# One matmul of 512 columns for the high and low parts of the input tokens in the last layer's feature-major products

## The chip, the cores and the metric

One core of a Trainium2 chip. The metric is the device time of one launch in microseconds (us). TensorE does the matrix products, ACT (ScalarE) and DVE (VectorE) the work on elements, SP issues the loads.

## The reference

Two layers act on 256 input tokens (x) and 256 context tokens, with 1024 features. A layer is: a gated feed-forward (hidden width 2816), a mixer with three branches, and a second feed-forward; each ends in a layer norm whose scale and shift come from a conditioning vector. In the last layer the context goes no further than the mixer's keys, values and states, so that all later products have only the 256 input tokens.

```python
for l in range(DEPTH):
    x = ffn_step(x); ctx = ffn_step(ctx)          # silu(h@a) * (h@g) @ w2
    zx, zc = split(mod(x) @ w_in), split(mod(ctx) @ w_in)
    a = gla_out(...) @ gla_proj                   # decay attention
    b = (z6 * short_conv(z7 * z8)) @ conv_proj    # short convolution over 3 tokens
    c = latent_attention(...) @ mla_proj
    x = norm(x + (sig(zg_a)*a + sig(zg_b)*b + sig(zg_c)*c) @ w_out)
    x = ffn_step(x)
```

## The kernel before

All products are made from high and low parts: a value v is split into h, its copy in the type that TensorE multiplies, and l = v - h. A product w·v is the sum wh·vh + wh·vl + wl·vh, three matmuls into the same PSUM tile (`mm3`, L227 to L235).

Weights come in tiles of 128 x 1024 values (512 KB). SP loads them in the order of use into five buffers. ACT makes the high part wh (L187) and DVE the low part wl (L188), into three buffers. The function `w` (L156), called before a tile's products, first issues the split of the tile that comes two later (`AHEAD` is 2). Nothing is reordered: each engine takes its instructions in the order in which the program issues them. An ACT or DVE operation that the program puts ahead of such a split therefore holds it back.

The activations hT are feature-major: 128 features by 512 tokens for each of 8 blocks k; columns X (0 to 255) are the input tokens, C (256 to 511) the context. `hTh` and `hTl` are two constant tiles. In the last layer, after its first feed-forward, `parts` is [X] and the products have 256 columns. `fm` (L246) runs a list of weight tiles: a tile of 256 output features by 4 blocks k has 8 pairs of output and block, so 16 products with wh and then 8 with wl. A tile for a gate has 128 outputs by 8 blocks, and as many products.

The stages of the last layer with such products, in order of time, and what follows their products:

- Gates (`gates`, L980): 3 x 8 outputs zg; ACT's tanh reads PSUM (L989). Those of latent attention fill in between its heads, those of decay attention between its outputs (`gla`), those of conv come inside its branch. The tanh is issued when the generator is next asked for a tile.
- Branches (`branch`, L992): 8 outputs each for latent attention (operand o), decay attention (yT) and conv (cv). DVE multiplies with the gate (L1010) and adds the branch before (L1012), whose rows SP loads from DRAM; in the conv branch ACT and DVE split the result (L243, L244). Beside the latent-attention branch the decays are made (L1079 to L1091, products dz).
- Conv (`conv`, L1022): four blocks of z7, z8 and z6, two outputs each. z7 is copied by ACT (L1034); z8 is multiplied by DVE (L1041), then ACT (L1043) and DVE (L1045, L1046) make the three-token filter; z6 is multiplied (L1051) and split (L240, L241).
- Feed-forward (`ffn_in`, L713): 11 blocks of four weight tiles (two for a, two for g), two outputs of each. ACT's Silu reads a (L739), DVE multiplies by g (L740), both split (L240, L241). In the block p = 1 DVE also renews the four pieces of the layer norm's result (L596, L597), one behind each weight tile.

Quantities that stay as they are: the first feed-forward and layer 0 (512 columns, `parts` is [X, C]), the mixer's first tiles, the query products, all token-major products (`tm_mm`).

Of the kernel before, what the change touches and what calls it, by code (L numbers as in the profile page):

```python
# [10 lines left out]
F32R = mybir.dt.float32r  # L11
U32 = mybir.dt.uint32
AF = mybir.ActivationFunctionType
ALU = mybir.AluOpType
# [96 lines left out]
class Core:  # L111
# [115 lines left out]
    def mm3(self, items, late):  # L227


        mm = self.nc.tensor.matmul  # L230
        for out, lhs, rhs, start, _ in items:
            mm(out, lhs[0], rhs[0], start=start, stop=False)  # L232
            mm(out, lhs[late], rhs[1 - late], start=False, stop=False)  # L233
        for out, lhs, rhs, _, stop in items:
            mm(out, lhs[1 - late], rhs[late], start=False, stop=stop)  # L235

    def split(self, hi, lo, src, scale=None):
        nc = self.nc
# [60 lines left out]
def build(ctx, tc, aps, out, plan=None):  # L299
# [200 lines left out]
        dve.tensor_scalar(ab0[:, 0, k], modT[0][:, 8 + 4 * half:12 + 4 * half, :], scalar1=1.0, scalar2=None, op0=ALU.add)  # L500
        dve.tensor_copy(ab0[:, 1, k], modT[0][:, k, :])

    hTh, hTl = g.const([P, 8, 512], "hTh", F32R), g.const([P, 8, 512], "hTl", F32R)
    hT = [(hTh[:, k, :], hTl[:, k, :]) for k in range(8)]

    def to_psum(z):

# [58 lines left out]
    def project_ln(op, nk, wsrc, tiles, l, i, gscale, inputs, keep, ab, kept=4):  # L566
# [142 lines left out]
        norm(d_)  # L709
        return [lambda: (put(c_), put(d_), onward([c_, d_]))], late  # L710


    def ffn_in(l, j, hT, tiles, gT, pend, late, opening=None):  # L713
        parts = parts_of(tiles)
        full = slice(0, parts[-1].stop)
        w13 = R["ffn_w13"][l, j]
        tiles_of = lambda c0, ps: g.fm_tiles(w13, c0, 8, g.pair_outs(ps), parts)
        psa, psg = {}, {}
        for p in range(NFB // 2):
            if p == 0 and opening is not None:  # L720
                psa[0], psg[0], psa[1] = [[g.PS("a") for _ in range(2)] for _ in range(3)]
                opening(tiles_of(0, psa[0]), tiles_of(DFF, psg[0]), tiles_of(256, psa[1]))
            else:
                tl = []
                if p not in psa:
                    psa[p] = [g.PS("a") for _ in range(2)]
                    tl += tiles_of(p * 256, psa[p])
                psg[p] = [g.PS("g") for _ in range(2)]
                tl += tiles_of(DFF + p * 256, psg[p])
                for n, _ in enumerate(g.fm(tl, hT, parts, group=3 if p == 0 and len(parts) > 1 else 1)):  # L730
                    if pend and n >= 1:
                        pend.pop(0)()
                    if late and p >= 1:
                        late.pop(0)()
                    elif p >= 2:
                        feed_share(4 * (NFB // 2 - 1 - p) + 2 - n)
            for b in range(2):
                s = g.T(name="sil")
                act.activation(s[:, full], psa[p][b][:, full], AF.Silu)  # L739
                dve.tensor_tensor(s[:, full], s[:, full], psg[p][b][:, full], op=ALU.mult)  # L740
                h, lo = g.pairs(1, "g")[0]
                g.split(h[:, full], lo[:, full], s[:, full])
                gT.append((h, lo))
        feed(10 ** 6)
# [6 lines left out]
    def mla(l, hT, tiles, W, krT, psq, o_all, filler, late):  # L751
# [202 lines left out]
        for i in range(nu + 2):  # L954
            if 1 <= i <= nu:
                live[i - 1][1]()
            if i < nu:
                hp, j, part = units[i]
                if i % (2 * np_) == 0:
                    if nxt is not None:  # L960
                        run_all(nxt)
                    nxt = heads(hp + 1, ds[hp + 1]) if hp + 1 < HM // 2 else None
                live[i] = [*score(ds[hp], j, part)]
            for _ in range((1, 2, 1, 0)[i % 4] if np_ == 2 else (3, 1)[i % 2]):
                if nxt is not None:
                    next(nxt, None)
                else:
                    next(filler, None)
            if i % (2 * np_) == 2 * np_ - 1 or i >= nu:
                next(filler, None)  # L970
            if i >= 2:
                hp, j, part = units[i - 2]
                if part is parts[0]:
                    o_all.append(g.pairs(1, "o")[0])
                values(ds[hp], j, part, live.pop(i - 2)[0], o_all[2 * hp + j])
            if 1 <= i <= nu:
                live[i - 1] = [prob_t(live[i - 1][0], units[i - 1][2])]
            renew(i % 2 == 1)

    def gates(l, bi, hT, tiles, W, zg):  # L980

        parts = parts_of(tiles)
        full = slice(0, parts[-1].stop)
        for b in range(8):
            ps = g.PS("zg")
            yield from g.fm(g.fm_tiles(W, C_ZG + bi * D + b * P, 8, [(0, P, ps)], parts, 128), hT, parts)
            th = g.U(name="th")
            f = 24 * l + 8 * bi + b
            act.activation(th[:, full], ps[:, full], AF.Tanh, scale=0.5, bias=hbg[:, f:f + 1])  # L989
            zg.append(th)  # L990

    def branch(l, op, proj, tiles, prev, outp, gts, zg, under=None, side=None):  # L992

        parts = parts_of(tiles)
        full = slice(0, parts[-1].stop)
        dst = None if outp is not None else tc.dram_tile([8, P, 512], F32, name=g.nm("mrg"))
        for p in range(4):
            while len(zg) < 2 * p + 2 and next(gts, gts) is None:
                pass
            if prev is not None:  # L1000
                pv = []
                for b in range(2):
                    u = g.U(name="prev")
                    sp.dma_start(u[:, full], prev[2 * p + b, :, full])
                    pv.append(u)
            psp = [g.PS("pj") for _ in range(2)]
            run_all(g.fm(g.fm_tiles(proj, p * 256, 8, g.pair_outs(psp), parts), op, parts), under and [under.pop(0)], 0, side)
            ms = [g.U(name="mg") for _ in range(2)]
            for b, m in enumerate(ms):
                dve.scalar_tensor_tensor(m[:, full], zg[2 * p + b][:, full], 1.0, psp[b][:, full], op0=ALU.add, op1=ALU.mult)  # L1010
                if prev is not None:
                    dve.tensor_tensor(m[:, full], m[:, full], pv[b][:, full], op=ALU.add)  # L1012
            for b, m in enumerate(ms):
                if outp is not None:
                    h, lo = g.pairs(1, "m")[0]
                    g.split(h[:, full], lo[:, full], m[:, full], 0.5)
                    outp.append((h, lo))
                else:
                    pool.dma_start(dst[2 * p + b, :, full], m[:, full])
        return dst  # L1020

    def conv(l, hT, tiles, W, side):  # L1022
# [5 lines left out]
        for p in range(4):  # L1028
            z = []
            ps = [g.PS("z7") for _ in range(2)]  # L1030
            run_all(g.fm(g.fm_tiles(W, C_Z7 + p * 256, 8, g.pair_outs(ps), parts), hT, parts), side=side)
            for b in range(2):
                t_ = g.T(name="z7")
                act.activation(t_[:, full], ps[b][:, full], AF.Copy)  # L1034
                z.append(t_)
            ps = [g.PS("z8") for _ in range(2)]
            run_all(g.fm(g.fm_tiles(W, C_Z8 + p * 256, 8, g.pair_outs(ps), parts), hT, parts), side=side)
            for b in range(2):
                y = z[b]
                u_ = g.U(name="cu")  # L1040
                dve.tensor_tensor(u_[:, full], y[:, full], ps[b][:, full], op=ALU.mult)  # L1041
                wv = lambda j: vec("conv_w", (l * 3 + j) * 8 + 2 * p + b)
                act.activation(y[:, full], u_[:, full], AF.Copy, scale=wv(1))  # L1043
                u3, y3 = r3(u_), r3(y)
                dve.scalar_tensor_tensor(y3[:, :, 1:], u3[:, :, :255], wv(0), y3[:, :, 1:], op0=ALU.mult, op1=ALU.add)  # L1045
                dve.scalar_tensor_tensor(y3[:, :, :255], u3[:, :, 1:], wv(2), y3[:, :, :255], op0=ALU.mult, op1=ALU.add)  # L1046
            ps = [g.PS("z6") for _ in range(2)]
            run_all(g.fm(g.fm_tiles(W, C_Z6 + p * 256, 8, g.pair_outs(ps), parts), hT, parts), side=side)
            for b in range(2):
                y = z[b]  # L1050
                dve.tensor_tensor(y[:, full], y[:, full], ps[b][:, full], op=ALU.mult)  # L1051
                h, lo = g.pairs(1, "cv")[0]
                g.split(h[:, full], lo[:, full], y[:, full])
                ops.append((h, lo))
        return ops

    def decay_weights(l):
# [36 lines left out]
    def gla(l, hT, tiles, W, gd, yT):  # L1094
# [128 lines left out]

        def to_yT(s):
            if not yT:
                yT.extend(g.pairs(8, "yT"))
            part = (X, C)[s]
            for k2 in range(4):
                ps = g.PS("yT")
# [249 lines left out]
```

## Time and profile before

| | us |
|---|---|
| median of 3 runs | 2694.52 (2691.72 to 2694.92) |
| profiled execution | 2696.85 |
| its span, first to last instruction | 2695.0 |
| PE busy (14243 products) | 2624.4, 97% |
| PEld busy (14243 weight loads) | 2235.4, 83% |
| DVE busy (2429 instructions) | 1601.8, 59% |
| ACT busy (1565 instructions) | 982.4, 36% |

PE is TensorE's matmuls, PEld its loads of stationary operands, which overlap with them. Matmuls are pipelined: one has a duration of 0.28 to 0.39 us, but the next starts earlier, so the rate is read from the starts. An engine's share of the span is an average over stages with different limits.

### The profile page before, as it was taken

The numbers are of one execution on the slowest core, as the hardware profiler recorded it, in microseconds if no ns is written. First come the engines' busy times: TensorE is split into PE (matmuls) and PEld (weight loads), VectorE is DVE, ScalarE is ACT, GpSimd is POOL, SyncE is SP. The second block draws the span as 40 slices with busy tenths as digits, with TensorE's granted clock in tenths as the row PEclk, the third lists the DMA queues.
The fourth block names the chain that finished last, engine by engine and source line by source line (L and its number), as shares of the span: only waits on it lengthen the run. The fifth ranks groups of instructions, "written<-read, shape, count | busy, mean of one in ns | idle before, by whom it ended". The sixth has DMA issues, their size and how long they took to land. (4 is left out here: it accounts for less than half of the span.)

```text
span 2695.0 us, 36231 instructions
## 1 busy us (share of the span) xinstructions
PE 2624.4 (97%) x14243; PEld 2235.4 (83%) x14243; DVE 1601.8 (59%) x2429; ACT 982.4 (36%) x1565; POOL 81.0 (3%) x149
## 2 busy tenths in 40 slices
PE   8999999999999999999999999998999999999998
PEld 6888789888887888878888788886789988998996
DVE  3666547765453767466666466554367745566655
ACT  2322224555332322333222142221245643454442
POOL 0000000000000000000000000000010000100000
PEclk9999999999999999999999999999999999999999
DMA  7554443223222645644454544464543343567555
GB/s 251 168 167 155 160 160 114 67 63 121 79 71 70 197 148 155 186 137 133 157 164 157 176 144 156 157 197 167 182 125 102 120 126 95 177 183 220 180 188 172
DMA packets 324609, 400.63 MB, mean 149 GB/s; under 512 B 28403, under 2 KB 241935, under 8 KB 324439
## 3 DMA queue, kind: packets, MB, share of 16 engines
q1 hardware_dynamic: 321623, 391.99, 46.3%
q0 software_dynamic: 2816, 6.34, 0.6%
q8 instruction: 111, 1.82, 0.3%
q14 instruction: 59, 0.48, 0.1%
HBM read 382.49 MB, written 15.77 MB: 148 GB/s over the span
## 5 line engine op out<-in xcount | busy, mean ns | idle before, releaser
L188 DVE TENSOR_TENSOR wl<-raw,wh 128x1024 fp32r<-128x1024 f32 (+1 forms) x529 | 638.5, 1214 | 545.6 <-ACT wh L187 348.3
L187 ACT ACTIVATE wh<-raw 128x1024 fp32r<-128x1024 f32 (+1 forms) x529 | 548.8, 1050 | 767.7 <-PE tm L233 272.9
L232 PE MATMUL a<-hTh,wh 128*128 128x512 f32 (+1 forms) x784 | 267.6, 355 | 6.9 <-DVE hTh L534 3.9
L440 DVE SCALAR_TENSOR_TENSOR acc<-raw,csil,acc 128x512 f32<-128x512 f32 x392 | 267.5, 745 | 0.0
L233 PE MATMUL a<-hTl,wh 128*128 128x512 f32 (+1 forms) x752 | 258.5, 356 | 1.5 <-DVE hTl L535 1.2
L232 PE MATMUL tm<-wh,gh 128*128 128x512 f32 x616 | 245.9, 399 | 6.6 <-ACT wh L187 6.6
L232 PE MATMUL g<-hTh,wh 128*128 128x512 f32 (+1 forms) x704 | 245.2, 359 | 0.0
L233 PE MATMUL tm<-wh,gl 128*128 128x512 f32 x616 | 243.9, 396 | 0.0
L233 PE MATMUL g<-hTl,wh 128*128 128x512 f32 (+1 forms) x688 | 240.2, 360 | 0.0
L232 PEld LDWEIGHTS a<-hTh,wh 128*128 128x128 f32 x784 | 151.8, 194 | 30.9 <-DVE hTh L534 4.8
L235 PE MATMUL tm<-wl,gh 128*128 128x512 f32 x616 | 163.4, 390 | 0.6 <-DVE wl L188 0.6
L233 PEld LDWEIGHTS a<-hTl,wh 128*128 128x128 f32 x752 | 145.6, 194 | 21.3 <-DVE hTl L535 2.8
L240 ACT ACTIVATE gh<-sil 128x512 fp32r<-128x512 f32 (+1 forms) x88 | 50.9, 578 | 302.1 <-DVE sil L740 302.1
L235 PE MATMUL a<-hTh,wl 128*128 128x512 f32 (+1 forms) x752 | 158.3, 353 | 0.8 <-DVE wl L188 0.8
L232 PEld LDWEIGHTS g<-hTh,wh 128*128 128x128 f32 x704 | 133.0, 189 | 20.7 <-issue 1.6
L235 PE MATMUL g<-hTh,wl 128*128 128x512 f32 (+1 forms) x688 | 149.5, 359 | 0.0
L232 PEld LDWEIGHTS tm<-wh,gh 128*128 128x128 f32 x616 | 118.7, 193 | 34.8 <-ACT wh L187 7.0
L233 PEld LDWEIGHTS g<-hTl,wh 128*128 128x128 f32 x688 | 130.0, 189 | 19.1
L235 PEld LDWEIGHTS a<-hTh,wl 128*128 128x128 f32 x752 | 126.6, 192 | 19.8 <-DVE wl L188 1.0
L233 PEld LDWEIGHTS tm<-wh,gl 128*128 128x128 f32 x616 | 118.5, 192 | 24.6
L235 PEld LDWEIGHTS tm<-wl,gh 128*128 128x128 f32 x616 | 115.4, 188 | 25.7 <-DVE wl L188 1.9
L235 PEld LDWEIGHTS g<-hTh,wl 128*128 128x128 f32 x688 | 117.9, 189 | 19.3
(323 smaller groups left out, 4706.3 us busy)
## 6 DMA issues: line engine op xcount, KB each, us to landing
raw<-in_ffn_w_dram SPq DMA_DIRECT2D x279, 512.0 KB
raw<-in_w_in_dram SPq DMA_DIRECT2D x156, 512.0 KB
raw<-in_ada_w_dram SPq DMA_DIRECT2D x128, 512.0 KB
raw<-in_w_out_dram SPq DMA_DIRECT2D x20, 512.0 KB
raw<-in_ada_w_dram SPq DMA_DIRECT2D x32, 256.0 KB
raw<-in_mla_proj_dram SPq DMA_DIRECT2D x16, 512.0 KB
raw<-in_gla_proj_dram SPq DMA_DIRECT2D x16, 512.0 KB
raw<-in_conv_proj_dram SPq DMA_DIRECT2D x16, 512.0 KB
```

What stands on the lines that cost most here:

```text
L187: nc.scalar.activation(hi[:, :n], raw[:, :n], AF.Copy)
L188: nc.vector.tensor_tensor(lo[:, :n], raw[:, :n], hi[:, :n].bitcast(F32), op=ALU.subtract)
L232: mm(out, lhs[0], rhs[0], start=start, stop=False)
L233: mm(out, lhs[late], rhs[1 - late], start=False, stop=False)
L235: mm(out, lhs[1 - late], rhs[late], start=False, stop=stop)
L240: nc.scalar.activation(hi, src, AF.Copy)
L440: dve.scalar_tensor_tensor(a, b, csil[:, k, s_:s_ + 1], a, op0=ALU.mult, op1=ALU.add)
```

## The change

`hTh` and `hTl` become the two halves of one tile `hT2`, so that for each block k one operand gives the 256 high and the 256 low columns of X, 512 in two runs. The operands o, yT and cv of the branches keep high and low part in one tile (`xpairs`), side by side. Where `parts` is [X], `fm_x` calls `fm_both`: wh multiplies both parts in one matmul of 512 columns, so that wh·vh is in columns 0 to 255 of the PSUM tile and wh·vl in 256 to 511; wl·vh is then added to the first half. `total` copies the second half out of PSUM with ACT and adds the first to it with DVE, and what read PSUM before reads the result from SBUF. The three products for a pair of output and block become two. The products that use `g.fm` with only X in the query path and those inside the heads stay.

```diff
+    def fm_both(self, tiles, act):
+        mm = self.nc.tensor.matmul
+        for pieces, ks, outs, nk, _ in tiles:
+            wh, wl = self.w(pieces, len(ks))
+            for c0, m, o in outs:
+                for kk, k in enumerate(ks):
+                    mm(o, wh[:, kk, c0:c0 + m], act[k][1], start=k == 0, stop=False)
+            for c0, m, o in outs:
+                for kk, k in enumerate(ks):
+                    mm(o[:, :256], wl[:, kk, c0:c0 + m], act[k][0], start=False, stop=k == nk - 1)
+            yield
+    def xpairs(self, n, name):
+        us = [self.U(F32R, name) for _ in range(n)]
+        return [(u[:, X], u[:, C], u) for u in us]
...
+    hT2 = g.const([P, 2, 8, 512], "hT2", F32R)
+    hTh, hTl = hT2[:, 0], hT2[:, 1]
+    hTx = [(hTh[:, k, X], hT2[:, :, k, X]) for k in range(8)]
...
+    def fm_x(tl, op, parts, group=1):
+        if len(parts) == 2:
+            return g.fm(tl, op, parts, group)
+        return g.fm_both(tl, hTx if op is hT else [(o[0], o[2]) for o in op])
+    def total(dst, ps, parts):
+        if len(parts) == 2:
+            return ps
+        act.activation(dst, ps[:, C], AF.Copy)
+        dve.tensor_tensor(dst, dst, ps[:, X], op=ALU.add)
+        return dst
...
-                act.activation(s[:, full], psa[p][b][:, full], AF.Silu)
-                dve.tensor_tensor(s[:, full], s[:, full], psg[p][b][:, full], op=ALU.mult)
+                a_ = total(s[:, X], psa[p][b], parts)
+                act.activation(s[:, full], a_[:, full], AF.Silu)
+                dve.tensor_tensor(s[:, full], s[:, full], total(s[:, C], psg[p][b], parts)[:, full], op=ALU.mult)
...
-            act.activation(th[:, full], ps[:, full], AF.Tanh, scale=0.5, bias=hbg[:, f:f + 1])
+            act.activation(th[:, full], total(th[:, X], ps, parts)[:, full], AF.Tanh, scale=0.5, bias=hbg[:, f:f + 1])
...
-                dve.scalar_tensor_tensor(m[:, full], zg[2 * p + b][:, full], 1.0, psp[b][:, full], op0=ALU.add, op1=ALU.mult)
+                dve.scalar_tensor_tensor(m[:, full], zg[2 * p + b][:, full], 1.0, total(m[:, X], psp[b], parts)[:, full], op0=ALU.add, op1=ALU.mult)
...
-                dve.tensor_tensor(u_[:, full], y[:, full], ps[b][:, full], op=ALU.mult)
+                dve.tensor_tensor(u_[:, full], y[:, full], total(u_[:, X], ps[b], parts)[:, full], op=ALU.mult)
...
-                dve.tensor_tensor(y[:, full], y[:, full], ps[b][:, full], op=ALU.mult)
+                dve.tensor_tensor(y[:, full], y[:, full], total(y[:, C], ps[b], parts)[:, full], op=ALU.mult)
```

## Rows read from the trace of the kernel before

**Rows 1.** Busy time by stretch: length, each engine (instructions), granted clock, DMA share, GB/s.

```profile
2135.00:2161.00 26.00, 25.43 (x203) 24.87 (x204) 20.05 (x29) 24.27 (x35) 3.34 (x6) 1.00 0.43 129
...
2416.00:2462.00 46.00, 46.00 (x386) 46.00 (x385) 29.03 (x39) 22.38 (x32) 0.00 (x0) 1.00 0.82 250
2495.00:2626.00 131.00, 130.85 (x1062) 130.34 (x1063) 76.98 (x98) 61.39 (x90) 0.00 (x0) 0.98 0.59 187
```

**Rows 2.** Timeline, feed-forward, PE: start us, duration, instruction, count [idle before <-releaser].

```profile
2566.26 1.12 PE L235 MATMUL g<-hTh,wl 128*128 128x256 f32 x8
2567.22 0.28 PE L232 MATMUL a<-hTh,wh 128*128 128x256 f32 x1
```

**Rows 3.** Timeline of PE, products of 512 columns in layer 0.

```profile
152.28 1.98 PE L235 MATMUL a<-hTh,wl 128*128 128x512 f32 x8
154.09 0.39 PE L232 MATMUL a<-hTh,wh 128*128 128x512 f32 x1
```

**Rows 4.** Timeline of PE, value products of latent attention, first and what follows.

```profile
2052.43 0.28 PE L232 MATMUL v<-wh,ckh 128*128 128x256 f32 x1
...
2055.30 0.28 PE L232 MATMUL zg<-hTh,wh 128*128 128x256 f32 x1
```

**Rows 5.** Groups by line and shape: busy us, mean ns | idle before and releaser.

```profile
L1034 ACT ACTIVATE z<-z 128x256 f32<-128x256 f32 x8 | 3.1, 384 | 6.5 <-PE z L235 6.1
...
L740 DVE TENSOR_TENSOR sil<-sil,g 128x256 f32<-128x256 f32 x20 | 8.4, 418 | 10.0 <-PE g L235 10.0
```

**Rows 6.** Timeline of DVE, ACT and PE behind a steady feed-forward block.

```profile
2567.01 0.42 DVE L740 TENSOR_TENSOR sil<-sil,g 128x256 f32<-128x256 f32 x1 [1.11 <-PE g L235]
...
2570.10 2.36 DVE L188 TENSOR_TENSOR wl<-raw,wh 128x1024 fp32r<-128x1024 f32 x2 [0.52 <-ACT wh L187]
...
2567.46 0.42 ACT L240 ACTIVATE gh<-sil 128x256 fp32r<-128x256 f32 x1 [2.55 <-DVE sil L740]
...
2568.70 0.42 ACT L240 ACTIVATE gh<-sil 128x256 fp32r<-128x256 f32 x1 [0.55 <-DVE sil L740]
2569.03 2.00 ACT L187 ACTIVATE wh<-raw 128x1024 fp32r<-128x1024 f32 x2
...
2572.98 0.28 PE L232 MATMUL g<-hTh,wh 128*128 128x256 f32 x1
```

**Rows 7.** Timeline of DVE, feed-forward block p = 1: first low part, and the multiplication.

```profile
2512.51 1.23 DVE L188 TENSOR_TENSOR wl<-raw,wh 128x1024 fp32r<-128x1024 f32 x1 [0.52 <-ACT wh L187]
...
2522.37 0.41 DVE L740 TENSOR_TENSOR sil<-sil,g 128x256 f32<-128x256 f32 x1
```

**Rows 8.** Two waits in PE's timeline, and busy time by stretch behind them.

```profile
1854.74 0.79 PE L232 MATMUL tm<-wh,gh 128*128 128x512 f32 x1 [6.60 <-ACT wh L187]
...
2312.75 0.39 PE L232 MATMUL pj<-yTh,wh 128*128 128x256 f32 x1 [1.10 <-ACT wh L187]
...
1856.00:1860.00 4.00, 4.00 (x11) 3.08 (x11) 2.60 (x4) 0.37 (x1) 0.00 (x0) 0.53 0.60 174
...
2310.00:2314.00 4.00, 2.90 (x24) 2.69 (x23) 2.63 (x5) 3.42 (x6) 0.00 (x0) 1.00 0.01 4
```

**Rows 9.** Timeline of PE, latent-attention branch, last weight tile.

```profile
2157.91 0.39 PE L232 MATMUL pj<-oh,wh 128*128 128x256 f32 x1 [0.57 <-ACT wh L187]
```

**Rows 10.** Timeline of ACT and DVE, end of decay attention.

```profile
2301.92 0.48 ACT L989 ACTIVATE th<-zg,hbg 128x256 f32<-128x256 f32 x1
...
2306.65 0.84 ACT L243 ACTIVATE yTh<-yT,hgn 128x256 fp32r<-128x256 f32 x2 [1.56 <-DVE yTl L244]
...
2311.64 2.96 ACT L187 ACTIVATE wh<-raw 128x1024 fp32r<-128x1024 f32 x3
...
2303.43 1.66 DVE L1222 SCALAR_TENSOR_TENSOR sr<-go,oss,sr 128x256 f32<-128x256 f32 x4 [5.62 <-POOL oss L749]
```

**Rows 11.** Timeline of ACT, conv branch, gate and next weight part.

```profile
2444.19 0.46 ACT L989 ACTIVATE th<-zg,hbg 128x256 f32<-128x256 f32 x1
2444.55 1.05 ACT L187 ACTIVATE wh<-raw 128x1024 fp32r<-128x1024 f32 x1
```

More of the change, by code (lines that the diff above doesn't have):

```diff
@@ L501, in mod_ab0 @@
         dve.tensor_copy(ab0[:, 1, k], modT[0][:, k, :])
-    hTh, hTl = g.const([P, 8, 512], "hTh", F32R), g.const([P, 8, 512], "hTl", F32R)
+    hT2 = g.const([P, 2, 8, 512], "hT2", F32R)
+    hTh, hTl = hT2[:, 0], hT2[:, 1]
     hT = [(hTh[:, k, :], hTl[:, k, :]) for k in range(8)]
+    hTx = [(hTh[:, k, X], hT2[:, :, k, X]) for k in range(8)]
     def to_psum(z):
@@ L710, in project_ln @@
         return [lambda: (put(c_), put(d_), onward([c_, d_]))], late
+    def fm_x(tl, op, parts, group=1):
+        if len(parts) == 2:
+            return g.fm(tl, op, parts, group)
+        return g.fm_both(tl, hTx if op is hT else [(o[0], o[2]) for o in op])
+    pairs_x = lambda n, name, parts: (g.pairs if len(parts) == 2 else g.xpairs)(n, name)
+    def total(dst, ps, parts):
[4 more added lines that the diff above has]
+        return dst
     def ffn_in(l, j, hT, tiles, gT, pend, late, opening=None):
@@ L729, in ffn_in @@
                 tl += tiles_of(DFF + p * 256, psg[p])
-                for n, _ in enumerate(g.fm(tl, hT, parts, group=3 if p == 0 and len(parts) > 1 else 1)):
+                for n, _ in enumerate(fm_x(tl, hT, parts, 3 if p == 0 else 1)):
                     if pend and n >= 1:
@@ L973, in mla @@
                 if part is parts[0]:
-                    o_all.append(g.pairs(1, "o")[0])
+                    o_all.append(pairs_x(1, "o", parts)[0])
                 values(ds[hp], j, part, live.pop(i - 2)[0], o_all[2 * hp + j])
@@ L985, in gates @@
             ps = g.PS("zg")
-            yield from g.fm(g.fm_tiles(W, C_ZG + bi * D + b * P, 8, [(0, P, ps)], parts, 128), hT, parts)
+            yield from fm_x(g.fm_tiles(W, C_ZG + bi * D + b * P, 8, [(0, P, ps)], parts, 128), hT, parts)
             th = g.U(name="th")
             f = 24 * l + 8 * bi + b
-            act.activation(th[:, full], ps[:, full], AF.Tanh, scale=0.5, bias=hbg[:, f:f + 1])
+            act.activation(th[:, full], total(th[:, X], ps, parts)[:, full], AF.Tanh, scale=0.5, bias=hbg[:, f:f + 1])
             zg.append(th)
@@ L1006, in branch @@
             psp = [g.PS("pj") for _ in range(2)]
-            run_all(g.fm(g.fm_tiles(proj, p * 256, 8, g.pair_outs(psp), parts), op, parts), under and [under.pop(0)], 0, side)
+            run_all(fm_x(g.fm_tiles(proj, p * 256, 8, g.pair_outs(psp), parts), op, parts), under and [under.pop(0)], 0, side)
             ms = [g.U(name="mg") for _ in range(2)]
             for b, m in enumerate(ms):
-                dve.scalar_tensor_tensor(m[:, full], zg[2 * p + b][:, full], 1.0, psp[b][:, full], op0=ALU.add, op1=ALU.mult)
+                dve.scalar_tensor_tensor(m[:, full], zg[2 * p + b][:, full], 1.0, total(m[:, X], psp[b], parts)[:, full], op0=ALU.add, op1=ALU.mult)
                 if prev is not None:
@@ L1030, in conv @@
             ps = [g.PS("z7") for _ in range(2)]
-            run_all(g.fm(g.fm_tiles(W, C_Z7 + p * 256, 8, g.pair_outs(ps), parts), hT, parts), side=side)
+            run_all(fm_x(g.fm_tiles(W, C_Z7 + p * 256, 8, g.pair_outs(ps), parts), hT, parts), side=side)
             for b in range(2):
                 t_ = g.T(name="z7")
-                act.activation(t_[:, full], ps[b][:, full], AF.Copy)
+                if len(parts) == 2:
+                    act.activation(t_[:, full], ps[b][:, full], AF.Copy)
+                else:
+                    total(t_[:, X], ps[b], parts)
                 z.append(t_)
             ps = [g.PS("z8") for _ in range(2)]
-            run_all(g.fm(g.fm_tiles(W, C_Z8 + p * 256, 8, g.pair_outs(ps), parts), hT, parts), side=side)
+            run_all(fm_x(g.fm_tiles(W, C_Z8 + p * 256, 8, g.pair_outs(ps), parts), hT, parts), side=side)
             for b in range(2):
@@ L1047, in conv @@
             ps = [g.PS("z6") for _ in range(2)]
-            run_all(g.fm(g.fm_tiles(W, C_Z6 + p * 256, 8, g.pair_outs(ps), parts), hT, parts), side=side)
+            run_all(fm_x(g.fm_tiles(W, C_Z6 + p * 256, 8, g.pair_outs(ps), parts), hT, parts), side=side)
             for b in range(2):
                 y = z[b]
-                dve.tensor_tensor(y[:, full], y[:, full], ps[b][:, full], op=ALU.mult)
-                h, lo = g.pairs(1, "cv")[0]
-                g.split(h[:, full], lo[:, full], y[:, full])
-                ops.append((h, lo))
+                dve.tensor_tensor(y[:, full], y[:, full], total(y[:, C], ps[b], parts)[:, full], op=ALU.mult)
+                hl = pairs_x(1, "cv", parts)[0]
+                g.split(hl[0][:, full], hl[1][:, full], y[:, full])
+                ops.append(hl)
         return ops
@@ L1225, in to_yT @@
             if not yT:
-                yT.extend(g.pairs(8, "yT"))
+                yT.extend(pairs_x(8, "yT", parts))
             part = (X, C)[s]
```

## The prediction

> **What bounds the kernel now.** I read the stages first: [rows 1] give the busy time of each engine in three stretches of the last layer. TensorE is busy for 130.85 of 131 us in the last feed-forward input and 46.00 of 46 in the conv branch, at a granted clock of 0.98 to 1.00 (the 2.4 GHz level). So the stretches that the change touches are bound by the stream of products, and a shorter stream is time won as long as the weight parts arrive in time. The latent-attention branch is different: ACT is busy 24.27 of 26 us there. Next I read the distance between products [rows 2, 3], then the waits of ACT and DVE, to see who has to finish before the weight parts of a coming tile are made, because the change lengthens just that.
>
> **The products.** Eight products of 256 columns take from 2566.26 to 2567.22, 0.120 us each [rows 2]; eight of 512 take from 152.28 to 154.09, 0.2265 us each [rows 3]. Two of 256 are 0.240, so a joined pair saves 0.0135 us, call it 0.0133: the cost that a product has beside its columns is paid once less. The new moving operand of hT is two runs of 256 lying 16 KB apart. Its nearest row is the value product, whose moving operand is two separated runs of 128: 24 of these take from 2052.43 to 2055.30, 0.120 each [rows 4], no more than one run does. I take 0.2265; the other end is 0.240, no gain at all. The pairs: 44 outputs in the feed-forward, 24 gates, 24 projections and 24 in conv, 116 outputs times 8 blocks, 928 pairs. A weight tile (8 pairs, 24 products) falls from 2.88 to 2.773 us, and 116 tiles save 12.4 us. The feed-forward's first two tiles or so run at the 1.2 GHz level (the 0.98 of [rows 1]); for these I count no saving, 0.25 us less.
>
> The Trainium skill (TensorE: Matmul & The Clock Gate, section Back-to-back issue gap) gives an isolated gap of N/2.4 + 2.5 ns, 109 and 216 ns. By it a pair saves 2.5 ns and the 928 save 2.3 us. The rows say 120 and 226.5, so I go by them.
>
> **What is added.** Each of the 116 outputs now needs an ACT copy of its low half out of PSUM and a DVE addition of the high half, before the operation that read PSUM directly; in conv 8 copies existed already. Both forms are in the trace: 0.384 and 0.418 us [rows 5]. That is about 41 us of ACT and 48 us of DVE in stretches where both have idle time. Their price lies in the order: ACT and DVE also make the weight parts, in program order, two tiles ahead.
>
> The hand-overs [rows 6]: DVE to ACT 0.45 us from start to start (multiplication 2567.01, split 2567.46), the operation and 0.03. ACT to DVE is the same (weight part of 1.06 at 2569.03, low part at 2570.10), so 0.41 behind a copy. The next independent operation on ACT comes 0.33 later (split 2568.70, weight part 2569.03), a second low part on DVE 1.13 later (two in 2.36). A dependent one on DVE I put at 0.45.
>
> *Feed-forward, steady block.* Call T the moment when the first gate output is complete: the fourth of the eight products of 2566.26 [rows 2] ends at 2566.26 + 0.36 + 0.28 = 2566.90. Now the weight part for the third tile after it starts at T + 2.13 and ends at T + 3.2; that tile starts at 2572.98, T + 6.08. After the change both outputs pass in series: copy 0.11, add 0.52, multiply 0.97, split 1.42, copy of the second a 1.75, add 2.21 (behind the low part on DVE), Silu 2.66, copy 2.95, add 3.36, multiply 3.81, split 4.26, weight part 4.59 to 5.65. The tile starts at T + 0.32 + 2 x 2.773 = 5.87. It just fits: no stall, but the slack is down from 2.9 to 0.2 us.
>
> *Feed-forward, second block.* Here DVE also does four renewals of the layer norm and is busy without a gap from 2512.51 to the multiplication at 2522.37, 9.86 us [rows 7]. In the changed kernel this run begins behind the longer chain of block one, at T + 5.67, so the first addition comes at T + 15.53, 4.4 us after that block's products are done. From there it is 0.45 to Silu, 0.29 to the copy, and 4.48 to the weight part, which ends at T + 21.8. The tile is due at T + 0.32 + 6 x 2.773 = 16.96. TensorE stands still for 4.95 us, once.
>
> *Clock.* Such a gap has a price of its own. After 6.60 us of waiting for a weight part the clock was at 1.2 GHz, still 0.53 granted in 1856 to 1860; after 1.10 us it stayed at 1.00 [rows 8]. About 5 us at half speed cost 2.5 us. Bounds: 0 and 3.4.
>
> *Latent-attention gates and branch.* The 8 gates are filler and save 0.85; I leave 0.3 of it, since each puts a DVE addition between ACT's operations. In the branch ACT is full, and a tile already waited 0.57 us for its weight part and started at 2157.91 [rows 9]. Four more copies go in front of that part, 4 times 0.33 minus some 0.43 that ACT waits there now: about 0.85 later. The tile starts that much later although it is due sooner, so the branch loses 0.7 instead of saving 0.85. The gap of some 2.3 us may lower the clock; half the cost of a short one, 0.9.
>
> *Decay-attention end and branch.* The first gate's addition is queued on DVE behind the four multiplications of 2303.43, so its tanh comes at 2305.46 instead of 2301.92 and the next weight parts 3.5 us later; the transposed outputs of 2306.65 shift by 1.9 us, and behind them the second gate passes copy and addition, so the weight part of 2311.64, for which the branch's second tile waits already (1.10 us, start 2312.75), comes 2.9 later [rows 8, 10]. Five tiles' savings are inside that wait; 11 others keep 1.2. Net +1.4, and 1.0 for the clock at a gap of 2.7 us.
>
> *Conv.* By the same hand-overs z8's two outputs, which pass ACT and DVE in series, stay in time by 0.45 with copy and addition in each. z6 comes 1.1 us late to DVE, behind two low parts, and runs eight hand-overs: the weight part ends at T + 6.1, due at 5.75, 0.45 late with TensorE's own take-up, in each of 4 blocks. Saving 2.56, loss 1.8: -0.8.
>
> *Conv branch.* Here splits, gate and weight part are one row of hand-overs (tanh 2444.19, weight part 2444.55 [rows 11]). With copies and additions a gate costs weight part 1.07, low part 1.13, addition 0.45, tanh 0.36: 3.01 against 2.773 for its products, and a block comes to about 11.8 us against 11.52 before. With the entry from conv: +1.0.
>
> **Sum.** Feed-forward -4.45 + 4.95 + 0.2 (its last block) = +0.7; latent attention -0.3 + 0.7; decay attention +1.4; conv -0.8; conv branch +1.0; clock 2.5 + 0.9 + 1.0 = 4.4. Together +7.1, of which I take 6.5, since early small slips are partly inside later ones. The profiled execution took 2696.85 (span 2695.0 and 1.85 around it), 2.33 above the median of 2694.52; so 2703.35 there and 2701.0 as a median.
>
> **Rivals.** *It cancels (2696).* The clock does not fall at any of the three gaps, and the gate rows overlap better than hop by hop: without the 4.4 and without the conv branch's 1.0 the sum is +1.7. For it: the clock stayed up after 1.10 us, and two of the three gaps lie between that and 6.60. Against it: the 4.95 us lie near the 6.60.
>
> *The stream's saving survives (2684).* If the weight parts stay ahead everywhere, only 12.2 us of saving is left, with perhaps 2 us lost: -10. One way to it: the copy need not wait for the last products, since the low half is complete 0.96 us before the high half. Against it: the high half's additions wait for the end anyway, and [rows 10] show ACT's reading of the other half of a bank ending its wait with DVE's read (2306.65), so halves are not independent. The 9.86 us run of DVE does not depend on it either.
>
> *No gain per pair (2711).* If reading two separate runs costs as much as the join saves, a pair gains nothing: 12.4 us are missing, though the weight parts then have 0.2 us more per two tiles and the losses of both conv stages (2.8) fall away: +6.5 + 12.4 - 2.8 = +16. For it: no row has runs 16 KB apart. Against it: [rows 4]. The Trainium skill's isolated gap (TensorE: Matmul & The Clock Gate, Back-to-back issue gap) would lead to the same case within some 2 us; [rows 2, 3] are against that.
>
> **Chances.** Forecast (slower, own range 2697 to 2708): 0.53, of which most lies above +5.4. Cancels: 0.26. Saving survives: 0.17. No gain per pair: 0.04. A measurement of this kernel can tell about 0.2%, 5.4 us. The range must reach into the second and third case at the bottom: 2687 to 2709. Faster 0.17; the cancelling case and the lower edge of the forecast, same 0.33; slower 0.50.
>
> **What would show it.** Right: joined products 0.2265 us apart; one gap of 4 to 6 us on TensorE in the third feed-forward block, released by an ACT weight part, with half clock behind it; ACT's weight parts in steady blocks starting 4.6 us after T; a wait above 3 us at the second tile of the decay-attention branch; conv-branch blocks of 11.8 us. Wrong: no gap above 2 us on TensorE in these stages, or additions that start before the renewals on DVE; then the time is below 2690. Distances of 0.24 us would mean the last rival.

## The result and the profile after

Before 2694.72 us (2691.72 to 2695.9, 4 runs), after 2719.44 (2718.61 to 2720.1, 4 runs): ratio 1.0093 (1.0081 to 1.0106), slower by 24.7 us where 6.5 were forecast, and outside the range. The profiled execution has a span of 2717.8 us, 22.8 more than before.

Where it went, by the start of the first product of each stage in the two timelines (a forecast for a branch includes the gates ahead of it):

| first product of | before | after | later by | lost since the row above | forecast, clock included |
|---|---|---|---|---|---|
| latent attention's gates | 2055.3 | 2053.7 | -1.6 | | |
| latent-attention branch | 2135.2 | 2140.7 | 5.5 | 7.1 | -0.3 |
| decay-attention branch | 2308.6 | 2314.7 | 6.1 | 0.6 | 1.6 |
| conv (z7) | 2347.4 | 2360.2 | 12.8 | 6.7 | 2.4 |
| conv branch | 2425.2 | 2436.5 | 11.4 | -1.4 | -0.8 |
| layer norm (zT) | 2484.4 | 2505.4 | 21.0 | 9.7 | 1.0 |
| feed-forward | 2494.8 | 2516.7 | 21.9 | 0.9 | 0 |
| end of the span | 2695.0 | 2717.8 | 22.8 | 0.9 | 3.2 |

So the loss lies in three places: latent attention's gates, the decay-attention branch and the conv branch. The stage conv itself gains. Two numbers are not the change's own: the -1.6 stands ahead of its first product, and the last 0.9 is too small by some 1.6. The low clock behind the feed-forward's first product cost 3.3 us of full-speed time in before's trace and 1.7 in after's, but also 1.7 in the trace of z3 below, which has before's products: it differs from one execution to the next.

The busy time by stretch, for the stages of [rows 1] at their new times (columns as there):

```profile
2131.00:2166.00 35.00, 30.89 (x160) 26.70 (x161) 26.50 (x43) 28.59 (x49) 3.75 (x6) 0.90 0.42 127
2438.00:2484.00 46.00, 39.70 (x205) 33.81 (x204) 27.39 (x45) 23.81 (x41) 0.00 (x0) 0.93 0.70 216
2517.00:2649.00 132.00, 127.36 (x711) 111.41 (x711) 91.07 (x137) 74.64 (x131) 0.00 (x0) 0.98 0.57 182
```

The conv branch, where TensorE was busy without a break, now has 6.3 us of 46 without a product, and a clock of 0.93. The joined products in the feed-forward, PE's timeline of after (they answer to [rows 2, 3]):

```profile
2594.50 2.00 PE L245 MATMUL a<-hT,wh 128*128 128x512 f32 x8
2596.34 1.12 PE L248 MATMUL a<-hT,wl 128*128 128x256 f32 x8
2597.30 2.00 PE L245 MATMUL g<-hT,wh 128*128 128x512 f32 x8
```

Eight joined products take 1.84 us, 0.230 each. A weight tile takes 2.79 on the mean of ten (2558.19 to 2586.12) against 2.88, so the product itself gains, a little less than forecast. The loss is in the waits of PE, here the main ones of after (in brackets the idle time and who ended it):

```profile
2114.30 2.12 PE L245 MATMUL zg<-hT,wh 128*128 128x512 f32 x8 [1.38 <-ACT wh L187]
2132.99 0.38 PE L232 MATMUL o<-pTh,vh 128*128 128x256 f32 x1 [3.11 <-ACT pTh L259]
2164.12 2.11 PE L245 MATMUL pj<-o,wh 128*128 128x512 f32 x8 [1.64 <-ACT wh L187]
2315.76 0.90 PE L245 MATMUL pj<-yT,wh 128*128 128x512 f32 x2 [0.52 <-DVE yT L263]
2317.17 1.44 PE L245 MATMUL pj<-yT,wh 128*128 128x512 f32 x5 [0.52 <-DVE yT L263]
2321.83 3.59 PE L245 MATMUL pj<-yT,wh 128*128 128x512 f32 x8 [2.27 <-ACT wh L187]
2357.11 2.11 PE L245 MATMUL pj<-yT,wh 128*128 128x512 f32 x8 [1.66 <-ACT wh L187]
2450.92 3.10 PE L245 MATMUL pj<-cv,wh 128*128 128x512 f32 x8 [2.65 <-ACT wh L187]
2479.26 3.60 PE L245 MATMUL pj<-cv,wh 128*128 128x512 f32 x8 [3.19 <-ACT wh L187]
2551.07 3.54 PE L245 MATMUL g<-hT,wh 128*128 128x512 f32 x8 [4.64 <-ACT wh L187]
```

Two smaller waits, 0.50 at 2343.72 and 0.41 at 2464.33, are left out. Three of these places were foreseen: 2321.83 (the decay-attention branch, where before waits 1.10 already), 2551.07 (the feed-forward) and 2164.12 (the latent-attention branch). Those at 2114.30, 2132.99 and 2357.11 and the two of the conv branch were not; they have two causes.

*The row of a gate.* ACT and DVE of after, two gates one behind the other in latent attention:

```profile
2126.79 0.37 ACT L746 ACTIVATE th<-zg 128x256 f32<-128x256 f32 x1
2127.65 0.51 ACT L1028 ACTIVATE th<-th,hbg 128x256 f32<-128x256 f32 x1 [0.49 <-DVE th L747]
2128.06 1.04 ACT L187 ACTIVATE wh<-raw 128x1024 fp32r<-128x1024 f32 x1
2129.01 0.36 ACT L746 ACTIVATE th<-zg 128x256 f32<-128x256 f32 x1
2130.73 0.51 ACT L1028 ACTIVATE th<-th,hbg 128x256 f32<-128x256 f32 x1 [1.36 <-DVE th L747]
2131.14 1.04 ACT L187 ACTIVATE wh<-raw 128x1024 fp32r<-128x1024 f32 x1
...
2132.35 1.07 ACT L259 ACTIVATE pTh<-pT 128x512 fp32r<-128x512 f32 x2
...
2129.14 1.23 DVE L188 TENSOR_TENSOR wl<-raw,wh 128x1024 fp32r<-128x1024 f32 x1 [1.52 <-ACT wh L187]
2130.28 0.41 DVE L747 TENSOR_TENSOR th<-th,zg 128x256 f32<-128x256 f32 x1
```

Weight part, low part, addition and tanh wait for one another: from one weight part to the next, 2128.06 to 2131.14, are 3.08 us. In program order the split of a coming tile stands ahead of the gate's addition on DVE, and the tanh that needs this addition stands ahead of the next weight part on ACT. Behind these gates and a second weight part comes pTh, the high part of the attention's probabilities, for which PE waits 3.11 us.

*The late loads.* SP, DVE and ACT of after, first block of the conv branch:

```profile
2435.44 1.04 ACT L187 ACTIVATE wh<-raw 128x1024 fp32r<-128x1024 f32 x1
...
2440.85 0.37 SPq L176 DMA_DIRECT2D raw<-in_w_in_dram  x1
2441.27 2.32 SPq L1043 DMA_DIRECT2D prev<-mrg  x2
...
2446.46 0.42 DVE L1051 TENSOR_TENSOR mg<-mg,prev 128x256 f32<-128x256 f32 x1 [2.58 <-DMA prev<-mrg]
...
2446.92 0.42 ACT L262 ACTIVATE mh<-mg 128x256 fp32r<-128x256 f32 x1 [3.82 <-DVE mg L1051]
...
2449.82 1.04 ACT L187 ACTIVATE wh<-raw 128x1024 fp32r<-128x1024 f32 x1
```

And SP and DVE of before at the same place:

```profile
2425.65 1.01 SPq L1004 DMA_DIRECT2D prev<-mrg  x2
...
2431.09 0.42 DVE L1012 TENSOR_TENSOR mg<-mg,prev 128x256 f32<-128x256 f32 x1
```

The loads of the previous sum (prev) stand on SP's queue behind a weight load that can go out only when a raw buffer is free, and DVE's low part frees it. Splits that come later thus make these loads later: before they went out 5.4 us ahead of their use, after so late that DVE waits 2.58 us for them in order, and with it mh, the next gate and the next weight part. The wait repeats as 0.67 and 3.12 in the next two blocks.

### The profile page after: what moved, and what is told of

Its sections match the earlier page's. It is cut to its first block, busy times and chain, and to the rows that moved or that the text cites. A ratio compares the mean times of both kernels' runs of the same rounds, so it can differ in the third digit from the quotient of the medians.

```text
span 2717.8 us, 34586 instructions
## 1 busy us (share of the span) xinstructions
PE 2623.6 (97%) x13315; PEld 2190.1 (81%) x13315; DVE 1643.4 (60%) x2545; ACT 1014.8 (37%) x1673; POOL 80.9 (3%) x149
## 5 line engine op out<-in xcount | busy, mean ns | idle before, releaser
L232 PE MATMUL a<-hT,wh 128*128 128x512 f32 (+1 forms) x608 | 221.4, 371 | 5.1 <-DVE hT L556 2.2
L233 PE MATMUL a<-hT,wh 128*128 128x512 f32 (+1 forms) x576 | 212.2, 374 | 1.1 <-DVE hT L557 1.0
L232 PE MATMUL g<-hT,wh 128*128 128x512 f32 (+1 forms) x528 | 202.0, 385 | 0.0
L233 PE MATMUL g<-hT,wh 128*128 128x512 f32 (+1 forms) x512 | 197.0, 386 | 0.0
L232 PEld LDWEIGHTS a<-hT,wh 128*128 128x128 f32 x608 | 115.6, 190 | 28.6 <-DVE hT L556 2.6
L235 PE MATMUL a<-hT,wl 128*128 128x512 f32 (+1 forms) x576 | 133.2, 374 | 2.3 <-DVE wl L188 2.3
L233 PEld LDWEIGHTS a<-hT,wh 128*128 128x128 f32 x576 | 109.5, 190 | 20.6 <-DVE hT L557 2.1
L235 PE MATMUL g<-hT,wl 128*128 128x512 f32 (+1 forms) x512 | 124.8, 386 | 0.0
L235 PEld LDWEIGHTS a<-hT,wl 128*128 128x128 f32 x576 | 103.2, 190 | 21.2 <-DVE wl L188 2.5
L232 PEld LDWEIGHTS g<-hT,wh 128*128 128x128 f32 x528 | 99.2, 188 | 20.7 <-issue 1.6
L233 PEld LDWEIGHTS g<-hT,wh 128*128 128x128 f32 x512 | 96.2, 188 | 19.0
L235 PEld LDWEIGHTS g<-hT,wl 128*128 128x128 f32 x512 | 95.2, 188 | 19.3
```

## The experiments

There are two theories at the start. T: the loss is the hand-overs alone (copy on ACT, addition on DVE), which hold weight parts behind them, and the joined products gain. R1: the joined products cost what is lost. R2 adds to T that part of the loss goes through the late loads on SP's queue. Each run is compared with before on its own chip; there before's median was between 2694.32 and 2694.72.

**x1_no_total: joined products without the hand-over.** The product wh·vl is computed and not added.

```diff
-        act.activation(dst, ps[:, C], AF.Copy)
-        dve.tensor_tensor(dst, dst, ps[:, X], op=ALU.add)
-        return dst
+        return ps
...
```

> The changed kernel with the joined 512-column products kept and the hand-over (total: copy on ACT, add on DVE) left out; the product of the high weights with the low input parts is computed but not added to the result. Theory T (the whole loss is the hand-overs, which hold back weight parts behind them on ACT and DVE, and the joined products gain 0.09 us on each of 116 tiles): about 2684, 10 below before. Rival R1 (the joined products themselves, with their two-run operand, cost what is lost): 2700 or more. Theory T with the late previous-sum loads (R2) makes the same number here, since without the hand-over the weight parts come early and so do those loads.

2686.43 (2685.22 to 2687.57), ratio 0.9968 (0.9958 to 0.9979): faster than before by 8, slower than the 2684 expected by 2.4. R1 falls: the whole loss, 33.0 us from here to after, comes with the hand-over.

**x2_total_alone: the old products with the hand-over.**

```diff
-        return g.fm_both(tl, hTx if op is hT else [(o[0], o[2]) for o in op])
+        return g.fm(tl, op, parts, 1)
...
-        act.activation(dst, ps[:, C], AF.Copy)
-        dve.tensor_tensor(dst, dst, ps[:, X], op=ALU.add)
+        act.activation(dst, ps[:, X], AF.Copy)
+        dve.tensor_tensor(dst, dst, ps[:, X], op=ALU.max)
```

> The kernel of before's three products of 256 columns each, with the hand-over alone added behind them (copy on ACT of the finished half, then a DVE operation over it and the finished half that leaves its value as it was; same instructions, order and sizes as in the changed kernel, operand tiles laid out as in the changed kernel). Theory T: 2720 to 2732, that is the changed kernel's 2719.4 plus up to the 10.4 that its joined products save, less what the slower products hide. R1: about 2695, since the products are the old ones.

2721.73 (2719.52 to 2723.02), 1.0101 (1.0086 to 1.0116). The hand-over makes the loss without any joined product. It is only 2.3 above after: where hand-overs set the pace, products that are shorter by 10 us gain little.

**x3_ffn_only: the change in the feed-forward alone** (in gates, branches and conv, `fm_x` is `fm` again and `total` gone).

> The change in the feed-forward part alone (32 of the 116 tiles); the attention and convolution stages are those of before. From the stage offsets of the two traces the feed-forward part lost 1.65 us: 2696.4 by that. By the terms of the prediction: saving 32 x 0.09 = 2.9, one stall of 4.6 and its clock 2: 2698. If the feed-forward part were the seat of the loss: 2705 or more.

2698.69 (2695.12 to 2700.07), 1.0015 (1.0006 to 1.0025): 4 slower. The tiles there are 44, not the 32 that the expectation counts: 44 x 0.09 = 4.0 saved, and with 4.64 of stall and 1.7 of clock 2.3 lost, which the interval holds. The feed-forward is the smaller part of the 24.7.

**x4_prev_early: after, with the loads of the previous sum ahead of the block's gates.**

```diff
-            while len(zg) < 2 * p + 2 and next(gts, gts) is None:
-                pass
             if prev is not None:
                 pv = []
...
                     sp.dma_start(u[:, full], prev[2 * p + b, :, full])
                     pv.append(u)
+            while len(zg) < 2 * p + 2 and next(gts, gts) is None:
+                pass
```

> The changed kernel, with the two loads of the previous sum in each block of a branch issued ahead of that block's gates instead of behind them, so that on SP's queue they stand ahead of the raw weight loads that wait for a buffer. R2 (the late loads make DVE wait in order, 6.4 us in the convolution's branch and up to 4.5 in the decay attention's, with the clock falling behind the waits): 2708 to 2712. Theory T without R2 (the copies, adds and tanhs alone hold the weight parts): 2718 to 2720.

2709.17 (2707.6 to 2711.94), 1.0056 (1.0041 to 1.0071): 10.3 back, as R2 expected. DVE's additions of the first output in the conv branch of this run:

```profile
2439.12 0.43 DVE L1051 TENSOR_TENSOR mg<-mg,prev 128x256 f32<-128x256 f32 x1
...
2450.96 0.42 DVE L1051 TENSOR_TENSOR mg<-mg,prev 128x256 f32<-128x256 f32 x1
...
2462.81 0.42 DVE L1051 TENSOR_TENSOR mg<-mg,prev 128x256 f32<-128x256 f32 x1
```

No wait for a load is left in this branch, and PE's waits of 2.65, 3.19 and 1.66 are gone. A block takes 11.84 and 11.85 us, the 11.8 of the prediction. In after the first block had 14.38 from weight part to weight part (2435.44 to 2449.82), 11.80 without DVE's 2.58.

**x5_renewals_spread: after, with one renewal of the layer norm to a block.**

```diff
                     if late and p >= 1:
-                        late.pop(0)()
+                        if len(parts) == 2 or n == 1:
+                            late.pop(0)()
```

> The changed kernel with the four renewals of the layer norm, which all stand in the second feed-forward block, spread one to a block over blocks two to five. The prediction's step (DVE's run of 9.86 us in the second block holds back the hand-over and with it a weight part; TensorE then stands 4.64 us and runs low behind it): the wait at the third block is gone or under 1 us, and the time is 4.6 for the wait and some 2 for the clock under the changed kernel: 2713. If the steady block's own chain of hand-overs makes the wait (its slack was worked out as 0.2 us), it comes back in other blocks: 2717 to 2720.

2716.04 (2714.94 to 2718.07), 1.0077 (1.0062 to 1.0092): 3.4 back, of 6.6 expected. PE's timeline of this run:

```profile
2547.79 2.12 PE L245 MATMUL g<-hT,wh 128*128 128x512 f32 x8 [0.67 <-ACT wh L187]
...
2584.49 2.14 PE L245 MATMUL g<-hT,wh 128*128 128x512 f32 x8 [0.79 <-ACT wh L187]
```

The wait of 4.64 is gone, so the four renewals in one block did cause it. Four waits of 0.67 to 0.79, one to a block (the first and the last are shown), stand in its place, together 3.03: a steady block has so little slack that one renewal (1.4 us of DVE) overruns it.

**y1_prev_early_tanh_late: x4, and each gate's tanh behind the next weight split.** Work put in `pend` is issued by `w` right behind the split.

```diff
-            act.activation(th[:, full], total(th[:, X], ps, parts)[:, full], AF.Tanh, scale=0.5, bias=hbg[:, f:f + 1])
+            t_ = total(th[:, X], ps, parts)
+            g.pend.append(lambda th=th, t_=t_, f=f: act.activation(th[:, full], t_[:, full], AF.Tanh, scale=0.5,
+                                                                  bias=hbg[:, f:f + 1]))
...
```

> The changed kernel with the early loads of the previous sum (the run before this kind: 2709.2) and with each gate's tanh on ACT put behind the next weight split instead of ahead of it, so that ACT's order is copy, weight part, tanh and no weight part waits for an addition on DVE. Theory (a gate costs a row of weight part, low part, addition and tanh, 3.08 us, against 2.79 of its products, and three gates in a row hold the weight and probability parts back): the 3.1 us wait at the o product and the low clock behind it in latent attention go, and the decay attention's end gets about 2 back: 2700 to 2704. If the row of the gates is not what holds them: 2708 to 2710.

2693.83 (2691.37 to 2695.99), 0.9996 (0.9986 to 1.0006): 15.3 back where 5 to 9 were expected. ACT's idle time ahead of the tanhs, from the answers on the tile th, first after, then y1 (us, number of waits):

```profile
  DVE th L747: 37.8, 24
```

```profile
  DVE th L754: 10.3, 6
```

All 24 gates made ACT wait for DVE; now 6 do. The row is broken, since copy, weight part and tanh stand in this order and the addition runs beside the weight part. ACT's timeline of y1, at gates of latent attention:

```profile
2109.91 1.07 ACT L194 ACTIVATE wh<-raw 128x1024 fp32r<-128x1024 f32 x1
2110.98 0.51 ACT L1036 ACTIVATE th<-th,hbg 128x256 f32<-128x256 f32 x1
2111.40 0.37 ACT L753 ACTIVATE th<-zg 128x256 f32<-128x256 f32 x1
2111.66 1.05 ACT L194 ACTIVATE wh<-raw 128x1024 fp32r<-128x1024 f32 x1
```

From one weight part to the next are 1.75 us instead of 3.08, and PE's waits of 1.38 and 3.11 are gone.

**z1_tanh_late_alone: after, with the late tanh alone** (the same edit, the loads where after has them).

> The changed kernel (2719.4) with only the tanh of each gate put behind the next weight split; the loads of the previous sum stand where the changed kernel has them. Early loads alone brought 10.3, and the late tanh on top of them 15.3. If the two are separate causes that add: 2719.4 - 15.3 = 2704. If the late loads are a consequence of the held splits (a raw buffer comes free with DVE's low part, which waits for the weight part that waits for the tanh): both are healed by the late tanh, 2694 to 2697.

2698.22 (2694.89 to 2702.79), 1.0017 (1.0008 to 1.0025): 21.2 back, close to neither number. So of 25.6 that both edits bring, the late tanh brings 21.2 alone and the early loads 10.3 alone; 5.9 is common to them, the part of the late loads that came from splits held by the tanh. The loads keep 4.4 of their own. The runs of x4, y1 and z1 scatter by 4 to 8 us, so the 5.9 and the 4.4 are good to some 3. SP, DVE and PE of z1 show them:

```profile
2434.65 1.00 SPq L1054 DMA_DIRECT2D prev<-mrg  x2
...
2440.08 0.43 DVE L1062 TENSOR_TENSOR mg<-mg,prev 128x256 f32<-128x256 f32 x1 [2.03 <-DMA prev<-mrg]
...
2443.48 2.11 PE L252 MATMUL pj<-cv,wh 128*128 128x512 f32 x8 [0.71 <-ACT wh L194]
```

The waits of DVE are 1.84 to 2.56 in all four blocks, those of PE behind them 0.71 to 1.50, 4.28 together.

**z3_before_prev_early: the control, the same move of the loads in before.**

> The kernel of before with the loads of the previous sum issued ahead of the block's gates. There the loads came 4.9 us ahead of their use and DVE's waits lay beside the products: 2694.5, no change within 2. If the early loads were a gain of their own, apart from the change: 2690 or less.

2693.76 (2691.86 to 2697.05), 1.0003 (0.9994 to 1.0011): nothing to be had, as expected. The loads were no limit until the change made them one.

**y2_and_ffn_order and y3_all_in_groups: a version that beats both.** y2 adds to y1, in the feed-forward, one renewal to a block, a's hand-over as soon as its products are done, two copies and then two additions, and the split of the gated product in `pend`; y3 groups copies and additions and puts the splits in `pend` in conv and the branches too. A part of y2's edit:

```diff
+                    if len(parts) == 1 and n == 1:
+                        sil = [g.T(name="sil") for _ in range(2)]
+                        totals([s[:, X] for s in sil], psa[p], parts)
+                        for s in sil:
+                            act.activation(s[:, X], s[:, X], AF.Silu)
...
```

> As the kernel with early loads and late tanh, and in the feed-forward part: renewals spread one to a block, the first two outputs' copies, additions and Silu as soon as their products are done, copies and additions of a pair of outputs grouped (two copies, then two additions), the split of the product put behind the next weight split. Theory: the 4.6 us wait and its low clock go and the feed-forward part keeps its 44 x 0.09 = 4.0: 5 to 7 below that kernel, some 2695 to 2698. If the feed-forward part's loss lies elsewhere: within 2 of it.

> As the kernel before it in this list, with the grouped copies and additions and the splits behind the next weight split also in the convolution and in the branches. Theory: with no weight part held by a hand-over the joined products' gain is what is left; the bound is the run without any hand-over, 2686.4: 2687 to 2692, faster than before. If copies and additions cost by their sheer time on ACT and DVE (in the latent-attention branch ACT was busy 24 of 26 us): 2694 or more.

y2 2687.98 (2685.08 to 2690.38), 0.9975 (0.9964 to 0.9986), 5.9 below y1. y3 2685.86 (2682.5 to 2688.04), 0.9964 (0.9951 to 0.9977): faster than before by 8.6 and than after by 33.6, and no slower than x1, which has no hand-over but the old order. What y3 adds to y2, 2.1, lies inside the intervals. y3's busy time in the conv branch:

```profile
2410.00:2456.00 46.00, 46.00 (x264) 40.39 (x263) 33.77 (x60) 28.34 (x50) 0.00 (x0) 1.00 0.85 257
```

TensorE is again busy without a break in the conv branch, though DVE does 33.77 us in it instead of the 29.03 of [rows 1]: here the sheer time of copies and additions costs nothing.

**z2_groups_old_products and z4_before_in_the_new_order: products or order?** z2 is y3 with the products and the hand-over of x2, z4 is y3 with the old products and no hand-over.

> The kernel with everything in groups (2685.9), with the three products of 256 columns of before in place of the joined one and the hand-over kept in kind and size (a copy of the finished half, and a DVE maximum with the finished half, which leaves the value as it was). What the joined products are worth where no hand-over holds a weight part: 116 tiles at 2.88 - 2.79 = 0.09 us, 10.4, so 2694 to 2697. If the order of the work made the gain and not the products: 2686 to 2689.

> The order of work of the kernel with everything in groups (late tanh and splits, early loads, renewals one to a block), but with the products of before and no hand-over. If the order only takes away what the hand-over brought: 2694 to 2696, as before. If the order is worth something by itself, and the joined products less: 2691 or below.

z2 2695.62 (2691.97 to 2696.49), 1.0005 (0.9996 to 1.0014); z4 2691.75 (2689.39 to 2697.22), 0.9995 (0.9986 to 1.0004). y3 lies 9.8 below z2, so the joined products are worth what 116 tiles of 0.09 us make, 10.4, once no hand-over holds a weight part. Against before, both z2 and z4 are within the noise. Against each other, on one chip with 11 runs each, they are not: z2's median is 3.9 above z4's and its mean 2.5. So the hand-over still costs some 2 to 4 us in the new order, and the order by itself, without it, may be worth 2.6 (z4's median against before's, which the interval does not bear out). What the change is worth in the new order is then y3 against z4, 5.9, and not the whole 8.6.

## Why the prediction was wrong

- *Direction and mechanism were right*: the stream of products became shorter, and weight parts held behind hand-overs cost more than that. What failed is where and how long they were held.
- *The products* were put at 0.2265 us each (the rows give 0.2263) and a saving of 12.4; they take 0.230 and save 10.4, measured as 8 in x1 and 9.8 between z2 and y3.
- *Steady feed-forward block*, put to fit with 0.2 us of slack and the weight part 4.59 behind T: right. In after the second g tile's low products start at 2601.93, so T is 2601.93 + 0.36 + 0.28 = 2602.57, and ACT's weight part starts at T + 4.57:

```profile
2601.93 1.11 PE L248 MATMUL g<-hT,wl 128*128 128x256 f32 x8
...
2602.60 0.38 ACT L746 ACTIVATE sil<-g 128x256 f32<-128x256 f32 x1
...
2607.14 2.94 ACT L187 ACTIVATE wh<-raw 128x1024 fp32r<-128x1024 f32 x3
```

- *The stall behind the renewals*, put at 4.95: 4.64, and x5 shows its cause. *Conv*, put at -0.8 with a stall in each block: -1.4, and PE's timeline shows no such stall there.
- *Decay-attention branch*, put at over 3 us at the second tile and 2.4 in all: 2.27 at that tile, and 6.7 in all. Two waits of 0.52 at the first tile, for the transposed outputs that the prediction saw shift, make 3.31 with it; the 0.50 and the 1.66 behind them come from the late loads below.
- *The step that failed first*: "The 8 gates are filler and save 0.85; I leave 0.3 of it". Latent attention lost 7.1 there. The row of hand-overs was priced, 3.01 us against a measured 3.08, but only in the conv branch. Where the filler asks for gates one after the other, each row also holds all that stands behind it on ACT, the next weight part and pTh: PE waits 1.38 and 3.11 us, and the clock falls. By y1 and z1 the gates' tanhs, of all three branches together, are the largest part of the loss, 15.3 to 21.2 of 33.0.
- *The step that failed second*: the conv branch at +1.0. The block of 11.8 was right (11.84 in x4), and the loads of the previous sum were left out, though the trace of before showed them on SP's queue. Their 5.4 us of lead were spent by splits that come later: 9.7 instead of 1.0, and in the decay-attention branch waits of 1.38 and 2.49 on DVE, from which PE's 0.50 at 2343.72 and 1.66 at 2357.11 come.
- *The clock* was put at 4.4 for three gaps; it fell behind five waits that the change made (2132.99, 2321.83, 2450.92, 2479.26, 2551.07). Busy time by stretch in after, the stretches with the fall behind three of them, and two with none:

```profile
2136.00:2140.00 4.00, 3.73 (x17) 3.38 (x17) 2.43 (x5) 1.86 (x4) 0.76 (x2) 0.50 0.27 79
...
2448.00:2452.00 4.00, 1.35 (x7) 1.00 (x6) 2.33 (x5) 2.41 (x5) 0.00 (x0) 0.97 0.59 199
2452.00:2456.00 4.00, 4.00 (x16) 3.46 (x16) 2.48 (x4) 3.35 (x4) 0.00 (x0) 0.60 0.38 131
...
2552.00:2556.00 4.00, 4.00 (x18) 3.32 (x17) 2.81 (x4) 2.24 (x3) 0.00 (x0) 0.73 0.57 174
...
2164.00:2168.00 4.00, 3.88 (x21) 3.36 (x22) 3.83 (x7) 3.97 (x8) 1.08 (x2) 1.00 0.37 104
2357.00:2361.00 4.00, 3.87 (x19) 3.19 (x20) 2.39 (x3) 2.65 (x6) 0.00 (x0) 1.00 0.40 82
```

One fall of this kind is worth 1.7 us: (1 - 0.97) x 4 + (1 - 0.60) x 4 for the gap at 2450.92; the longest, in latent attention, 3.4 by the same sum over 2132 to 2144; the five together some 10. The sum also counts low clock while TensorE still stood. By the products alone, the eight behind 2551.07 took 3.38 instead of 1.84 to the start of the next (2554.45), 1.54 more. The feed-forward's 2.5 is too high by some 0.8, and behind the gap at 2164.12, for which 0.9 was counted, the clock stayed up. The clock's share follows the gaps; no run holds the gaps and changes the clock alone, so it stays worked out, not shown.
- *The rivals*: "It cancels" asked that the clock stay up at all three gaps; it fell at two of them. "No gain per pair" is refuted by z2 against y3. "The stream's saving survives" (2684) names about what y3 then reached, 2685.9, by another order of the same work. The way to it that the rival gave, copies that start early, was not the one: in after the copies wait for the last products of their output, those with wl (L248; 0.77 us at 2442.24).

## What to carry to other kernels

When an operation is put between a product and its reader, price the engine's queue behind it, not only its duration: follow program order on every engine until the row closes on itself, then ask which loads leave only when that row frees a buffer. Hand-overs that cross two engines go in groups (all copies, then all additions), and what depends on them goes behind the next prefetch work; in y3 this turned 25 us of loss into 9 of gain, 3 of which may be the order's own, with the same number of products, copies and additions. A lead of a load is slack like any other, and a change of order elsewhere may spend it.

## What was not expected of the hardware

A joined product takes 0.230 us whether its operand is two runs 16 KB apart (hT, 2594.50 above) or one run (cv), as PE's timeline of y3 shows:

```profile
2431.33 2.00 PE L252 MATMUL pj<-cv,wh 128*128 128x512 f32 x8
2433.17 1.11 PE L255 MATMUL pj<-cv,wl 128*128 128x256 f32 x8
```

From start to start both are 1.84 us for eight, so the distance of the runs is free, and the 0.004 us over the 0.226 of [rows 3] are not the price of the second run; what they are, no run here tells. The Trainium skill (TensorE: Matmul & The Clock Gate, section Back-to-back issue gap) gives 216 ns for 512 columns and 109 for 256 as the isolated gap; the traces show 230 and 119 to 120, so a pair gains some 0.01 us here and not the 2.5 ns that the formula makes of it.

TensorE's clock stayed at the 2.4 GHz level (granted 1.00) behind waits of 1.38, 1.64 and 1.66 us and fell towards the 1.2 GHz level behind waits of 2.27 (with two of 0.52 shortly ahead), 2.65, 3.11, 3.19 and 4.64.
